# Which engine makes the low parts of the weights in the attention and the mixing of a two-layer hybrid block: one VectorE operation a block in place of two on GpSimd

## The chip, the core and the metric

The kernel runs on one core of a Trainium2 chip. The metric is the device time in microseconds (us) of one execution. Five engines work side by side, each through its own queue in order: TensorE (PE in the profile; its weight loads are PEld), VectorE (DVE), ScalarE (ACT), GpSimd (POOL) and SyncE (SP), which here issues all DMA transfers.

## The reference, cut to what matters

```python
for l in range(2):                                   # x: 512 tokens x 1024
    h = rmsnorm(x, norm_mix[l]);  z = h @ w_in[l]    # 1024 -> 6936 columns, split into 15 parts
    o_nsa  = nsa(...)          # 8 heads of 64; three softmax branches: compressed keys, selected, window
    o_ret  = retention(...)    # 4 heads, chunks of 128
    o_conv = conv_module(...)  # depthwise, 31 taps, 512 channels, layernorm, silu
    merged = sum_n sigmoid(m_g[n]) * (o_n @ w_branch[l, n])
    x = x + merged @ w_out[l]
    h2 = rmsnorm(x, norm_mlp[l])
    x = x + square(relu(h2 @ w_ff1[l])) @ w_ff2[l]   # 1024 -> 4096 -> 1024
return rmsnorm(x, norm_final)
```

All of it is in float32.

## The kernel before

**Products in three passes.** A float32 operand is split into a high part, its copy in the type fp32r, and a low part, the operand minus the high part. A product is then high x high, high x low and low x high. `proj` (L157) does this for one output block of 128 columns: 8 chunks of 128 rows, three matmuls of 128x512 for each, 24 in all; a branch weight has 4 chunks and 12 matmuls.

**Weight blocks.** `wblock` (L153) fetches a block (`raw`, L136, tile `wr`, by a DMA of the SP queue) and splits it (`wsplit`, L142): ScalarE writes the high part `wh` (L145), then another engine writes the low part `wl`. `lo_engine` (L134) says which: GpSimd in two halves (L148), VectorE in one operation (L150). `wr`, `wh` and `wl` have three buffers each, so a block's high part waits until TensorE is done with the block three before.

```python
nc.scalar.activation(h, t, AF.Copy)                              # L145
if lo_engine[0] is nc.gpsimd:
    for k in (slice(0, nk // 2), slice(nk // 2, nk)):
        nc.gpsimd.tensor_sub(l[:, k], t[:, k], f(h[:, k]))       # L148
else:
    nc.vector.tensor_sub(l, t, f(h))                             # L150
```

GpSimd is set at the start, VectorE for one block of the first convolution input (L310), and VectorE for the feed-forward part (L799), with GpSimd again behind it (L819).

**A layer, in order.** Norm and split of x (`norm_split`, L209); convolution inputs and retention (L304 to L438); compressed keys, keys and values (`compress`, L485; L550 to L577); attention (L620 to L760), eight rounds of a head pair's half, each with two branches of scores, softmax and weighted values; mixing of the three branches and the output projection (L762 to L793); feed-forward (L796 to L818).

**What lies inside the attention.** For each branch of a head: scores on TensorE (`sc`), bias and row minimum on VectorE (L712), exponent on ScalarE (L714), the normaliser on VectorE (`gate_over`, L624: L627 to L629, 128x4 elements), scaling on ScalarE (L719), transposes on TensorE (`tp`, L722), the transposed block split by ScalarE (L727) and VectorE (L728, `pt`), then the weighted values on TensorE (`av`). Between them stand independent projections (`fill`, L474, called by `more`, L745): gates (`gate`, L444: projection, L448 on VectorE, tanh on ScalarE) and the retention's branch (`mix`, L456). VectorE also does the convolution there, one tap an operation (`conv_taps`, L329, L338), spread behind other work, and the split queries (L657).

**What sets the order.** The program is recorded through a framework whose scheduler orders the instructions of every engine; `tc.issue_after` binds some of them to others. A change of engine for one operation therefore moves others too. TensorE's work does not change in amount.

Of the kernel before, what the change touches and what calls it, by code (L numbers as in the profile page):

```python
# [66 lines left out]
def block_kernel(ctx: ExitStack, tc: tile.TileContext, a, out):  # L67
    nc = tc.nc
# [18 lines left out]
    def new_pool(name, side="left"):  # L87
        return tc.tile_pool(name=name, bufs=1, side=side, reuse_waits="tile")
# [45 lines left out]
    lo_engine = [nc.gpsimd]  # L134
# [74 lines left out]
    def norm_split(x, gain, first_time=False):  # L209

        pairs, acc = [], None
        for c in range(KC):
            h, l = tl(base, "X", 16, dtype=FR), tl(base, "X", 16, dtype=FR)
            at = nc.scalar.activation(h, x[c], AF.Copy, scale=gain[:, c:c + 1])  # L214
            nc.vector.scalar_tensor_tensor(l, x[c], gain[:, c:c + 1], f(h), op0=OP.mult, op1=OP.subtract)
            pairs.append((h, l))
            if c == (KC - 1 if first_time else 0):
                last = at
        with tc.issue_after(last.ins):
            for c in range(KC):  # L220
                s = tmp()
                if first_time and c < 3:
                    nc.gpsimd.tensor_mul(s, x[c], x[c])
                else:
                    nc.scalar.activation(s, x[c], AF.Square)
                if acc is not None:
                    (nc.vector if c == KC - 1 or first_time else nc.gpsimd).tensor_add(s, s, acc)  # L227
                acc = s
        rs4 = rsqrt_rows(column_sums(acc), 1.0 / D)
        rs = tl(base, "rs", 1)  # L230
        nc.scalar.activation(rs, rows_to_bcast(rs4), AF.Copy)
        return pairs, rs4, rs
# [37 lines left out]
    for l in range(DEPTH):  # L270
# [346 lines left out]
        normed = conv_norm()  # L617


        a2 = open_pools.enter_context(new_pool(f"late{l}"))  # L620
        phase = ExitStack()
        ap = phase.enter_context(new_pool(f"att{l}"))
# [173 lines left out]
        phase = ExitStack()  # L796
        fp = phase.enter_context(new_pool(f"ff{l}"))
        X, rs4, rs = norm_split(xT, par(8, 8))
        lo_engine[0] = nc.vector  # L799
        for q in range(4):  # L800
            A = []
            for m in range(KC):
# [86 lines left out]
```

## Time and profile before

| | us |
|---|---|
| median of 3 runs | 1793.1 |
| lowest and highest run | 1789.49 and 1793.3 |
| the profiled execution's own time | 1793.25 |
| its span, first to last instruction | 1791.5 |

Busy time says how long an engine had an instruction under way; the granted clock (PEclk, or `clock`) is the share of full speed that TensorE was given, 1.00 for 2.4 GHz and 0.50 for 1.2 GHz, averaged over a stretch. Over the whole span it is 0.989. Times of rows are counted from the start of the span. In layer 0 the stretch from 196 to 222 us is the passage from the keys and values into the attention, 222 to 380 us the body of the attention, 380 to 455 us its tail, where the projections between run out, and 455 to 545 us the mixing; in layer 1 the same stretches are 1075 to 1102, 1102 to 1260, 1260 to 1337 and 1337 to 1425 us.

### The profile page before, as it was taken

The numbers are of one execution on the slowest core, as the hardware profiler recorded it, in microseconds if no ns is written. First come the engines' busy times: TensorE is split into PE (matmuls) and PEld (weight loads), VectorE is DVE, ScalarE is ACT, GpSimd is POOL, SyncE is SP. The second block draws the span as 40 slices with busy tenths as digits, with TensorE's granted clock in tenths as the row PEclk, the third lists the DMA queues.
The fourth block names the chain that finished last, engine by engine and source line by source line (L and its number), as shares of the span: only waits on it lengthen the run. The fifth ranks groups of instructions, "written<-read, shape, count | busy, mean of one in ns | idle before, by whom it ended". The sixth has DMA issues, their size and how long they took to land.

```text
span 1791.5 us, 23230 instructions
## 1 busy us (share of the span) xinstructions
PE 1750.2 (98%) x8592; PEld 1469.7 (82%) x8592; DVE 1101.9 (62%) x1979; ACT 775.0 (43%) x1421; POOL 504.8 (28%) x420
## 2 busy tenths in 40 slices
PE   8899899999999999999999999999999999999997
PEld 7788788887888888888898888888778888888886
DVE  6976978776764344434459768878768443434344
ACT  4433466675443232323434344667644442323241
POOL 4454444322581000000255544343327500000000
PEclk9999999999999999999999999999999999999999
DMA  4222623321553232333322232232236332332321
GB/s 166 89 86 64 198 95 107 112 95 65 205 184 105 94 94 94 96 95 101 133 101 89 89 119 92 95 126 98 83 122 227 122 94 95 94 96 93 106 85 69
DMA packets 70801, 195.82 MB, mean 109 GB/s; under 512 B 8944, under 2 KB 9328, under 8 KB 70688
## 3 DMA queue, kind: packets, MB, share of 16 engines
q1 hardware_dynamic: 70688, 194.34, 33.5%
q8 instruction: 68, 1.11, 0.3%
q14 instruction: 45, 0.37, 0.1%
HBM read 177.51 MB, written 19.42 MB: 110 GB/s over the span
## 4 chain that ended last, share of the span: by engine, by line
PE 68%; issue 20%; DVE 10%; ACT 1%; DMA 1%; SPq 0%; POOL 0%; POOLq 0%; DVEq 0%; ACTq 0%
PE mm L109 59%; PE sc L109 3%; PE av L109 3%; DVE yc L338 3%; PE tp L722 2%; PE tp L109 1%; DVE qk L386 1%; DVE XP L500 0%; DVE pc L684 0%; DVE rr L364 0%; DVE QS L657 0%; DVE s L712 0%; DVE pt L728 0%; DVE g L448 0%; DVE kv L563 0%
## 5 line engine op out<-in xcount | busy, mean ns | idle before, releaser
L109 PE MATMUL mm<-X,wh 128*128 128x512 f32 x2432 | 779.5, 396 | 12.5 <-ACT X L214 6.0
L148 POOL TENSOR_TENSOR wl<-wr,wh 128x512 fp32r<-128x512 f32 (+2 forms) x344 | 440.1, 1302 | 542.8 <-ACT wh L145 526.8
L145 ACT ACTIVATE wh<-wr 128x1024 fp32r<-128x1024 f32 (+2 forms) x301 | 296.0, 986 | 650.9 <-PE mm L109 522.1
L109 PEld LDWEIGHTS mm<-X,wh 128*128 128x128 f32 x2432 | 456.0, 190 | 102.2 <-ACT X L214 6.0
L109 PE MATMUL mm<-X,wl 128*128 128x512 f32 x1216 | 480.7, 395 | 0.0
L109 PEld LDWEIGHTS mm<-X,wl 128*128 128x128 f32 x1216 | 230.5, 190 | 45.3
L338 DVE SCALAR_TENSOR_TENSOR yc<-u,ccol,yc 128x512 f32<-128x512 f32 x240 | 213.0, 889 | 1.5
L150 DVE TENSOR_TENSOR wl<-wr,wh 128x1024 fp32r<-128x1024 f32 x129 | 158.1, 1226 | 38.2 <-ACT wh L145 38.2
L109 PE MATMUL mm<-bo,wh 128*128 128x512 f32 x512 | 160.6, 392 | 0.0
L109 PE MATMUL mm<-fa,wh 128*128 128x512 f32 x512 | 160.2, 395 | 0.0
L806 DVE SCALAR_TENSOR_TENSOR t<-mm,rs 128x512 f32<-128x512 f32 x64 | 43.9, 691 | 161.6 <-PE mm L109 156.1
L206 POOL TENSOR_TENSOR n<-n,mhalf 128x4 f32<-128x4 f32 x15 | 17.4, 1159 | 371.9 <-DVE n L204 371.9
L227 POOL TENSOR_TENSOR t<-t,t 128x512 f32<-128x512 f32 x18 | 27.4, 1523 | 333.7 <-DVE wl L150 314.4
L109 PE MATMUL mm<-kv,wh 128*128 128x512 f32 x384 | 119.7, 390 | 0.0
L109 PEld LDWEIGHTS mm<-fa,wh 128*128 128x128 f32 x512 | 96.1, 188 | 23.2
L109 PEld LDWEIGHTS mm<-bo,wh 128*128 128x128 f32 x512 | 96.1, 188 | 19.5
L728 DVE TENSOR_TENSOR pt<-tp,pt 128x256 fp32r<-128x256 f32 (+1 forms) x192 | 71.2, 375 | 65.0 <-ACT pt L727 64.3
L109 PE MATMUL mm<-fa,wl 128*128 128x512 f32 x256 | 100.6, 395 | 0.0
L109 PE MATMUL mm<-bo,wl 128*128 128x512 f32 x256 | 100.0, 391 | 0.0
L714 ACT ACTIVATE s<-s,n 128x128 f32<-128x128 f32 (+3 forms) x128 | 71.3, 558 | 43.9 <-DVE n L712 43.4
L109 PE MATMUL mm<-wh,X 128*128 128x256 f32 (+1 forms) x480 | 90.2, 287 | 0.0
L727 ACT ACTIVATE pt<-tp 128x256 fp32r<-128x256 f32 (+1 forms) x192 | 63.7, 340 | 58.6 <-PE tp L722 42.6
(219 smaller groups left out, 2417.9 us busy)
## 6 DMA issues: line engine op xcount, KB each, us to landing
wr<-in_w_dram SPq DMA_DIRECT2D x128, 512.0 KB, 3.6
wr<-in_w_f_dram SPq DMA_DIRECT2D x87, 512.0 KB, 3.3
wr<-in_w_b_dram SPq DMA_DIRECT2D x48, 256.0 KB, 2.7
wr<-in_w_t_dram SPq DMA_DIRECT2D x16, 512.0 KB, 3.4
gd<-g SPq DMA_DIRECT2D x32, 256.0 KB, 2.0
g<-gd SPq DMA_DIRECT2D x32, 256.0 KB, 4.1
wr<-in_w_o_dram SPq DMA_DIRECT2D x16, 512.0 KB, 3.6
md<-g SPq DMA_DIRECT2D x16, 256.0 KB, 2.9
```

What stands on the lines that cost most here:

```text
L109: return nc.tensor.matmul(o, l, r, start=start, stop=stop)
L145: nc.scalar.activation(h, t, AF.Copy)
L148: nc.gpsimd.tensor_sub(l[:, k], t[:, k], f(h[:, k]))
L150: nc.vector.tensor_sub(l, t, f(h))
L227: (nc.vector if c == KC - 1 or first_time else nc.gpsimd).tensor_add(s, s, acc)
L338: nc.vector.scalar_tensor_tensor(yc[c], x, w, yc[c], op0=OP.mult, op1=OP.add)
L386: nc.vector.tensor_sub(QLr[h][half], pt[nat], f(QHr[h][nat]))
L714: nc.scalar.activation(s, s, AF.Exp, scale=-1.0, bias=mx[:, i:i + 1], accum_out=den[:, i:i + 1])
L722: nc.tensor.transpose(pt[:, k * P:(k + 1) * P], cols[i][:, k * P:(k + 1) * P], ident)
L727: nc.scalar.activation(vh, src, AF.Copy)
L728: low = nc.vector.tensor_sub(vl, src, f(vh))
L806: nc.vector.scalar_tensor_tensor(t, pf, 0.0, rs, op0=OP.max, op1=OP.mult)
```

## The change

`lo_engine` is set to VectorE ahead of the attention instead of ahead of the feed-forward part. Lines 620 to 799 of the kernel before have numbers that are one higher behind the change.

```diff
         normed = conv_norm()
 
 
+        lo_engine[0] = nc.vector
         a2 = open_pools.enter_context(new_pool(f"late{l}"))
         phase = ExitStack()
         ap = phase.enter_context(new_pool(f"att{l}"))
...
         X, rs4, rs = norm_split(xT, par(8, 8))
-        lo_engine[0] = nc.vector
         for q in range(4):
```

On GpSimd 344 instructions of L148 become 112; on VectorE 129 of L150 become 245. The 116 blocks that move, 58 a layer, are 70 of 128x1024 and 46 of 128x512: the queries, all but the first block pair of the retention's mixing, the gates that are computed ahead, the branch weights and the output projection. Instructions of TensorE, ScalarE and SP are the same in number.

On VectorE, layer 0, at the passage into the attention, before (`yc` is a convolution tap, `XP`, `m` belong to the compressed keys, `kv` are keys and values):

```order
L338 SCALAR_TENSOR_TENSOR yc_261<-u_952,ccol,yc_261 128x512 x3
L500 TENSOR_TENSOR XP_1742<-E_1735,pcol 128x16x31
L338 SCALAR_TENSOR_TENSOR yc_261<-u_952,ccol,yc_261 128x512
...
L513 TENSOR_TENSOR m_1687<-m_1687,tp_1670 128x62
L573 SCALAR_TENSOR_TENSOR kv_2068<-mm_1947,n_177,kv_2068 128x4x64
```

and with the change:

```order
L150 TENSOR_TENSOR wl_2100<-wr_2097,wh_2099 128x1024
L338 SCALAR_TENSOR_TENSOR yc_261<-u_952,ccol,yc_261 128x512 x2
L500 TENSOR_TENSOR XP_1742<-E_1735,pcol 128x16x31
L338 SCALAR_TENSOR_TENSOR yc_261<-u_952,ccol,yc_261 128x512
...
L513 TENSOR_TENSOR m_1687<-m_1687,tp_1670 128x62
L150 TENSOR_TENSOR wl_2260<-wr_2257,wh_2259 128x1024
L573 SCALAR_TENSOR_TENSOR kv_2068<-mm_1947,n_177,kv_2068 128x4x64
```

The low parts of the first two queries now stand ahead of the operations on the values (L573); the rest of the order there is as it was.

On VectorE, layer 0, in the tail of the attention, before (`g` is a gate, `pt` a transposed block, `on` the end of a round):

```order
L728 TENSOR_TENSOR pt_4122<-tp_4147,pt_4121 128x2x128
L448 TENSOR_TENSOR g_4525<-mm_4493,rs_179 128x512
L728 TENSOR_TENSOR pt_4122<-tp_4147,pt_4121 128x256
L338 SCALAR_TENSOR_TENSOR yc_263<-u_1476,ccol,yc_263 128x512
L728 TENSOR_TENSOR pt_4235<-tp_4237,pt_4234 128x128
L338 SCALAR_TENSOR_TENSOR yc_263<-u_1476,ccol,yc_263 128x512
L739 TENSOR_TENSOR on_3984<-t_4202,av_3985 64x512
```

and with the change:

```order
L729 TENSOR_TENSOR pt_4096<-tp_4121,pt_4095 128x2x128
L448 TENSOR_TENSOR g_4493<-mm_4462,rs_179 128x512
L150 TENSOR_TENSOR wl_4631<-wr_4628,wh_4630 128x512
L729 TENSOR_TENSOR pt_4096<-tp_4121,pt_4095 128x256
L338 SCALAR_TENSOR_TENSOR yc_263<-u_1476,ccol,yc_263 128x512
L729 TENSOR_TENSOR pt_4208<-tp_4210,pt_4207 128x128
L338 SCALAR_TENSOR_TENSOR yc_263<-u_1476,ccol,yc_263 128x512
L740 TENSOR_TENSOR on_3959<-t_4175,av_3960 64x512
```

A low part has come in right behind the operation that empties a gate's projection (L448), ahead of the next transposed block; the rest is as it was.

## Rows read from the trace of the kernel before

**Rows 1.** The page's first part: busy time, share of the span and number of instructions of each engine.

```profile
PE 1750.2 (98%) x8592; PEld 1469.7 (82%) x8592; DVE 1101.9 (62%) x1979; ACT 775.0 (43%) x1421; POOL 504.8 (28%) x420
```

**Rows 2.** The busy time of each engine in the stretches around the change. Columns: the stretch, its length, then for each engine its busy time with the number of instructions, the granted clock, the share of the DMA engines and GB/s.

```profile
196.00:222.00 26.00, 21.31 (x124) 18.87 (x124) 25.47 (x35) 5.70 (x14) 10.29 (x8) 0.93 0.55 168
222.00:380.00 158.00, 156.48 (x808) 132.19 (x807) 125.28 (x353) 109.20 (x267) 59.02 (x51) 1.00 0.32 104
380.00:455.00 75.00, 71.00 (x351) 58.31 (x350) 51.51 (x134) 44.50 (x109) 20.30 (x16) 0.95 0.22 72
455.00:545.00 90.00, 90.00 (x401) 73.62 (x400) 61.23 (x78) 39.93 (x60) 63.12 (x50) 1.00 0.60 203
...
1075.00:1102.00 27.00, 24.98 (x138) 22.61 (x136) 26.59 (x39) 7.11 (x17) 11.20 (x9) 0.87 0.32 102
1102.00:1260.00 158.00, 157.10 (x807) 132.79 (x807) 125.48 (x356) 107.94 (x265) 58.71 (x51) 1.00 0.32 103
1260.00:1337.00 77.00, 73.00 (x365) 60.19 (x364) 51.38 (x128) 46.98 (x115) 20.65 (x17) 0.96 0.24 81
1337.00:1425.00 88.00, 88.00 (x384) 71.37 (x383) 59.31 (x76) 36.90 (x56) 62.78 (x51) 1.00 0.60 195
```

**Rows 3.** TensorE's waits between 196 and 222 us: who waited for whom, us in total, times, the longest.

```profile
PE mm L109 <- ACT G L575: 4.7, 1, 4.7
```

**Rows 4.** Who waited for GpSimd's low parts (L148) in the whole span: us, times.

```profile
  ACT wh L145: 27.0, 14
  PEld mm L109: 0.6, 3
```

**Rows 5.** GpSimd's low parts by form, in the body (first two rows) and in the tail (last two) of layer 0's attention. Columns: line, engine, operation, tiles, shapes, number | busy us, mean ns of one | idle time before them and its releaser.

```profile
L148 POOL TENSOR_TENSOR wl<-wr,wh 128x512 fp32r<-128x512 f32 x36 | 49.0, 1384 | 74.4 <-ACT wh L145 74.4
L148 POOL TENSOR_TENSOR wl<-wr,wh 128x256 fp32r<-128x256 f32 x12 | 9.1, 777 | 21.9 <-ACT wh L145 21.9
...
L148 POOL TENSOR_TENSOR wl<-wr,wh 128x512 fp32r<-128x512 f32 x12 | 17.0, 1438 | 38.0 <-ACT wh L145 33.2 <-PE tp L722 4.7
L148 POOL TENSOR_TENSOR wl<-wr,wh 128x256 fp32r<-128x256 f32 x4 | 3.3, 846 | 16.9 <-ACT wh L145 16.9
```

**Rows 6.** VectorE's low parts of 128x1024 and, as the nearest operation of 128x512, the low part of an activation in the feed-forward part; whole span, columns as above.

```profile
L150 DVE TENSOR_TENSOR wl<-wr,wh 128x1024 fp32r<-128x1024 f32 x129 | 158.1, 1226 | 38.2 <-ACT wh L145 38.2
...
L113 DVE TENSOR_TENSOR fa<-t,fa 128x512 fp32r<-128x512 f32 x32 | 21.8, 692 | 1.7 <-ACT fa L112 1.7
```

**Rows 7.** Four kinds of VectorE operation in the body of layer 0's attention, columns as above.

```profile
L338 DVE SCALAR_TENSOR_TENSOR yc<-u,ccol,yc 128x512 f32<-128x512 f32 x40 | 34.0, 849 | 0.0
L657 DVE TENSOR_TENSOR QS<-tq,QS 64x512 fp32r<-64x512 f32 x8 | 8.5, 1063 | 0.7 <-ACT QS L656 0.4
...
L627 DVE TENSOR_SCALAR n<-n 128x4 f32<-128x4 f32 x18 | 7.6, 440 | 4.3 <-ACT s L714 4.1
...
L629 DVE SCALAR_TENSOR_TENSOR n<-G,n 128x4 f32<-128x4 f32 x18 | 5.9, 335 | 0.2
```

**Rows 8.** The same four over the whole span: shortest, median and longest in ns, then first and last start in us.

```profile
L338 DVE SCALAR_TENSOR_TENSOR yc<-u,ccol,yc x240: 729/745/1866, 35.3 to 1313.8; 128x512 f32<-128x512 f32 x120
...
L657 DVE TENSOR_TENSOR QS<-tq,QS x16: 684/963/1810, 223.1 to 1231.4; 64x512 fp32r<-64x512 f32 x16
...
L627 DVE TENSOR_SCALAR n<-n x48: 152/170/1254, 230.0 to 1304.5; 128x4 f32<-128x4 f32 x48
...
L629 DVE SCALAR_TENSOR_TENSOR n<-G,n x48: 147/161/1254, 230.6 to 1304.9; 128x4 f32<-128x4 f32 x48
```

**Rows 9.** VectorE's instructions in order of time at the passage into layer 0's attention: start and length in us, engine, line, operation.

```profile
194.41 1.65 DVE L338 SCALAR_TENSOR_TENSOR yc<-u,ccol,yc 128x512 f32<-128x512 f32 x1
196.09 1.64 DVE L563 TENSOR_TENSOR kv<-t,kv 64x512 fp32r<-64x512 f32 x1
...
200.01 2.03 DVE L500 TENSOR_TENSOR XP<-E,pcol 128x496 f32<-128x496 f32 x1
201.96 1.71 DVE L338 SCALAR_TENSOR_TENSOR yc<-u,ccol,yc 128x512 f32<-128x512 f32 x1
203.59 0.97 DVE L500 TENSOR_TENSOR XP<-E,pcol 128x496 f32<-128x496 f32 x1
```

**Rows 10.** VectorE's longest waits in the body of layer 0's attention: who for whom, us in total, times, the longest.

```profile
DVE pt L728 <- ACT pt L727: 15.7, 18, 2.0
DVE s L712 <- PE sc L109: 6.5, 7, 2.9
DVE n L627 <- ACT s L714: 4.1, 5, 1.0
```

**Rows 11.** Stretches of 20 us outside the attention in which VectorE was busy for 17.9 to 18.9 us; columns as in rows 2.

```profile
60.00:80.00 20.00, 18.25 (x93) 14.76 (x91) 18.37 (x29) 11.08 (x20) 11.16 (x10) 1.00 0.25 80
120.00:140.00 20.00, 20.00 (x104) 17.17 (x103) 17.97 (x28) 9.28 (x17) 12.91 (x11) 1.00 0.27 87
940.00:960.00 20.00, 19.46 (x124) 17.55 (x123) 18.12 (x38) 10.89 (x20) 10.13 (x11) 1.00 0.24 79
960.00:980.00 20.00, 19.78 (x97) 16.32 (x96) 17.96 (x23) 6.32 (x10) 11.31 (x8) 1.00 0.28 93
...
1060.00:1080.00 20.00, 20.00 (x144) 19.05 (x142) 18.80 (x20) 12.37 (x20) 10.18 (x8) 1.00 0.49 166
```

## The prediction

> **What bounds the kernel now.** I began with the busy times of the page: TensorE is under way for 98% of the span and VectorE for 62% [rows 1]. That is an average over stages, so the stretches around the change come next [rows 2]. The reader should see three different things there. In the mixing TensorE is busy for all of 90 and all of 88 us: nothing on another engine costs time. In the body of the attention it is busy for 156.5 and 157.1 of 158 us, and VectorE for 125.3 and 125.5 of them, which is 79%: TensorE is the bound, with VectorE not far behind. In the passage into the attention and in its tail TensorE loses time: 26 - 21.3 = 4.7 us and 27 - 25.0 = 2.0 us at the passages, 75 - 71 = 4.0 us and 77 - 73 = 4.0 us in the tails, and the granted clock is 0.93, 0.87, 0.95 and 0.96 there instead of 1.00.
>
> Then I looked at who waits for the low parts that are to move. TensorE's weight loads waited for GpSimd three times, 0.6 us in all; ScalarE waited 27 us in 14 cases for a buffer [rows 4], and it is not the bound. So a faster low part buys nothing by itself. What the change can buy or cost lies on VectorE: what it takes on, what it is freed of, and whether TensorE then waits for it.
>
> **What is moved, and its price.** Each layer moves 35 blocks of 128x1024 and 23 of 128x512. VectorE makes a 128x1024 low part in 1.226 us; for 128x512 I take 0.692 us, the nearest operation of that shape [rows 6]. That is 35 x 1.226 + 23 x 0.692 = 58.8 us a layer on VectorE, 117.6 us in all, in place of two GpSimd operations a block. Where it falls decides.
>
> **What VectorE is freed of.** Some VectorE operations take much longer in some places than in others. In the body a convolution tap takes 849 ns on average [rows 7] against a median of 745; the 128x4 steps L627 and L629 take 440 and 335 ns [rows 7] against medians of 170 and 161, with single cases of 1254 ns; a split query takes 1063 ns against a shortest of 684 [rows 8]. A step on four columns that lasts 1.25 us is not at work; it is as long as GpSimd's halves of 1.38 us on average [rows 5], and I read it as held up by them. With no low parts on GpSimd in the body this goes: 40 x 0.104 + 18 x 0.270 + 18 x 0.174 + 8 x 0.379 = 15.2 us of VectorE time a layer. The bounds are 0 (they are held by something else) and 15.2; I take it whole, since both the short and the long values of the same shape are there.
>
> **Body of the attention.** Per layer 36 / 2 = 18 large and 12 / 2 = 6 small blocks lie there [rows 5]: 18 x 1.226 + 6 x 0.692 = 26.2 us. Net of the 15.2 us VectorE goes from 125.3 to 136.3 of 158 us, 86%. What does TensorE lose at such a load? The nearest rows are the stretches with VectorE at 90%: 17.97 of 20 us with no loss of TensorE and 17.96 with 0.22 us; over all five stretches of 90 to 94% the loss is 1.75 + 0 + 0.54 + 0.22 + 0 = 2.51 us, 0.50 each [rows 11]. For 158 us that is 7.9 x 0.50 = 4.0 us against the 1.5 us lost now, so +2.5 us a layer at the high end; the two nearest rows give 7.9 x 0.11 = 0.9 us, no more than now. The low end is -1.5 us, all of today's loss gone. I take 0. If this cover is gone, each us that VectorE is late is a us of TensorE's.
>
> **Passage into the attention.** TensorE stands still for 4.7 us in layer 0, waiting for the gates' tanh on ScalarE (L575), which frees the accumulators [rows 3]; that stands behind VectorE's operations on the values (L573), and VectorE is busy for 25.5 of 26 us [rows 2]. The order of the change puts two large low parts ahead of the first L573: + 2 x 1.226 = 2.5 us. Four operations ahead of it are slow now: two taps of 1.65 and 1.71 us, an L563 of 1.64 us and an L500 of 2.03 us whose twin takes 0.97 [rows 9]. Beside 0.745 us for a tap [rows 8], 0.69 us for the L563 (from the split query of the same shape, shortest 684 ns [rows 8]) and 0.97 us, the excess is 0.90 + 0.96 + 0.95 + 1.06 = 3.9 us. So 3.9 - 2.5 = 1.4 us off the wait. Bounds: -4.7 us (the wait goes) and +2.5 us (the excess stays). For layer 1, where the loss is 2.0 us, I take 0.
>
> **Tail.** 6 large and 2 small blocks a layer [rows 5] are 8.7 us more on VectorE, which has 51.5 of 75 us [rows 2]. There is room, but here the chain transposes, L727, L728, weighted values is bare, and the order puts the low parts between its links, each behind an L448. Bounds: 0 (each lies under a gate's 24 matmuls) and 8.7 us a layer (all on the chain). As most stand behind a gate's projection while another runs, I take one of the eight on the chain: 8.7 / 8 = 1.1 us a layer, 2.2 us in all.
>
> **Mixing.** 16 small and 8 large are at most 16 x 0.692 + 8 x 1.226 = 20.9 us on top of 61.2 of 90 us. TensorE is full there; I cost it at nothing, and 4.5 x 0.50 = 2.3 us a layer [rows 11] if the cover fails.
>
> On the splitting of the work: the Trainium skill (Perfetto Trace Analysis, Optimizing Scalar/DVE Operations) says that where such an engine is not saturated but makes others wait, breaking an operation up can let work finish sooner; the change does the opposite, one operation a block for two. By that rule TensorE could begin a block half an operation earlier before, and the sum would be that of the third rival; by the row of three waits in all it is nothing, and the sum goes by the row.
>
> **The sum.** Against the profiled execution, 1793.25 us, which is 0.15 us above the median: - 1.4 + 0 + 2.2 + 0 gives **1794.0 us**, no change. About 0.2%, 3.6 us, is what a measurement of this kernel can tell from none.
>
> **The rivals.** First, faster: the relief reaches TensorE where it stands still. The passages lose 4.7 + 2.0 us, and the clock there costs 26 x 0.07 + 27 x 0.13 = 5.3 us more [rows 2]; all of it gone is -12 us, 1781, and half, **1787 us**. For it: the slow VectorE operations stand directly ahead of the L573 for which TensorE waits [rows 3, 9]. Against it: the two new low parts stand there too.
>
> Second, slower: VectorE becomes the bound in the body. Its idle time there is 158 - 125.3 = 32.7 us, 26.3 of them waits for ScalarE and TensorE [rows 10]; its low parts wait for ScalarE as well, 38.2 us for 129, 0.30 us each [rows 6], 7.1 us for 24. If none of these 39.8 us is filled by the new work, VectorE needs 136.3 + 39.8 = 176 us, 18 us a layer more than TensorE, 1830. It decides where less than 18 / 39.8 = 45% is filled; at a third filled it is 136.3 + 26.5 = 162.8 us, 4.8 us a layer, and with it **1804 us**. For it: the queue is in order, and a low part that waits for its high part holds every score and transposed block behind it. Against it: the longest group is 18 waits of 0.9 us on average, so one low part of 1.2 us fills one whole, and the rows at 90% lose little [rows 11].
>
> Third, each of the 116 blocks makes TensorE wait for the half that it once had early, 1.226 / 2 = 0.61 us: at most +71 us, **1864 us**. Rows 4 speak against it. That the change doesn't do what it says is excluded by the order: 232 instructions have left GpSimd and 116 have come to VectorE.
>
> **How the numbers follow.** No change 0.39, the first rival 0.30, the second 0.29, the third 0.02. Faster by over 0.2% is the first, 0.30; slower the second and third, 0.31. The forecast's own range is 1790 to 1797 us; the range for 8 in 10 takes in most of the first two rivals and leaves out their ends, some 0.1 each way: 1784 to 1807 us.
>
> **What would show it.** Right: VectorE busy for about 136 us of a body that is still 158 us, L627 and L629 near 0.17 us and taps near 0.75 us there; TensorE's wait for L575 near 3.3 us; two tails together longer by some 2 us. Wrong: a body of over 161 us with TensorE waiting for L713 (the row minimum, L712 before) or L729; a passage without a wait and a clock of 1.00 there; taps as slow as before.

## The result, and the profile after

The median after is **1804.7 us** (5 runs, 1803.95 to 1809.72) against 1793.1 us before: ratio **1.0071**, 95% interval 1.0059 to 1.0083. That is slower. The forecast's time, 1794.0 us, did not come; the time of its second rival, 1804 us, did, and lies in the range. The profiled execution took 1803.95 us with a span of 1802.2 us, 10.7 us over that of before.

Three marks on TensorE's queue say where: the first scores with compressed keys (`sc<-kc`), the first product of the mixing (`mm<-os`), the first product that reads activations of the feed-forward part (`mm<-fa`). "Mixing" between the last two marks is longer than the 90 us of [rows 2]: it takes in the norm and the first quarter of the feed-forward's first products. All times in this table are from TensorE's rows of the two timelines, in us.

| | before | after | difference |
|---|---|---|---|
| start to first scores, layer 0 | 222.8 | 220.5 | -2.3 |
| attention, layer 0 and 1 | 236.5, 236.1 | 239.7, 241.3 | +3.2, +5.2 |
| mixing, layer 0 and 1 | 134.0, 134.3 | 135.9, 135.9 | +1.9, +1.6 |
| last `mm<-fa` of layer 0 to first scores of layer 1 | 287.4 | 288.0 | +0.6 |

This adds up to 10.2 of the 10.7 us. The attention carries 8.4, the mixing 3.5, and the passages give 1.7 back.

Not all of that is the change, for each length carries TensorE's clock as well. In before, the granted clock is 0.50 for 6.8 us of each attention; in after it is so for 6.8 us of layer 1's and not in layer 0's. The stretch in layer 0 of before:

```profile
438.60:445.40 6.80, 6.33 (x28) 5.64 (x26) 2.85 (x9) 1.60 (x5) 0.00 (x0) 0.50 0.07 28
```

At half speed 6.8 us cost some 3.4 (an estimate). With such stretches taken out the attentions are 6.6 and 5.2 us longer than before. The 2.3 us at the start are not the change alone either: the wait in the passage is 1.5 us shorter, but TensorE also comes to it 0.9 us earlier, and at 80 us, far ahead of the change, it had the lower clock for 6.8 us before and for 3.4 us after.

The page's first part of after [rows 1 of before]: GpSimd loses 285 us of busy time, VectorE gains only 30, though its low parts (L150) take 116.8 us more. Its other operations are shorter by 72 us in sum; the rest is overlap of neighbouring operations, which busy time counts once.

```profile
PE 1750.1 (97%) x8592; PEld 1466.2 (81%) x8592; DVE 1131.9 (63%) x2095; ACT 776.6 (43%) x1421; POOL 220.0 (12%) x188
```

The stretches of after, as [rows 2] (the last two shifted to where the tail and the mixing of layer 1 now lie):

```profile
196.00:222.00 26.00, 22.78 (x132) 20.15 (x131) 24.09 (x43) 8.49 (x18) 0.31 (x1) 0.93 0.66 197
222.00:380.00 158.00, 154.66 (x795) 130.12 (x795) 127.64 (x366) 106.02 (x258) 0.94 (x3) 1.00 0.32 104
380.00:455.00 75.00, 67.48 (x345) 54.78 (x344) 56.56 (x145) 46.74 (x115) 0.00 (x0) 1.00 0.18 60
455.00:545.00 90.00, 88.27 (x393) 71.80 (x392) 66.48 (x98) 37.41 (x57) 9.75 (x6) 1.00 0.62 202
...
1102.00:1260.00 158.00, 156.48 (x800) 131.56 (x799) 129.71 (x366) 103.65 (x255) 0.94 (x3) 1.00 0.33 107
1260.00:1346.00 86.00, 79.20 (x394) 64.92 (x393) 61.62 (x153) 51.91 (x126) 0.00 (x0) 0.96 0.22 69
1346.00:1436.00 90.00, 88.27 (x387) 71.52 (x386) 66.56 (x98) 36.43 (x55) 11.54 (x7) 1.00 0.60 194
```

In the body VectorE has hardly more to do than before, 127.6 against 125.3 us, while TensorE has lost 1.8 us; in the tail TensorE is idle 7.5 of 75 us (4.0 before), and the mixing has a gap of 1.7 us where it had none. TensorE's waits of after in layer 0 from 222 to 460 us:

```profile
PE sc L109 <- DVE n L713: 5.6, 6, 1.6
PE av L109 <- DVE pt L729: 2.5, 4, 0.7
PE av L109 <- ACT pt L728: 1.2, 2, 0.7
PE mm L109 <- DVE u L590: 0.9, 1, 0.9
PE av L109 <- DVE on L740: 0.7, 1, 0.7
```

and of before in the same stretch:

```profile
PE sc L109 <- DVE n L712: 3.1, 5, 1.0
PE av L109 <- DVE on L739: 1.0, 1, 1.0
PE av L109 <- DVE pt L728: 0.5, 1, 0.5
PE av L109 <- ACT pt L727: 0.5, 1, 0.5
```

10.9 us against 5.1 (and 0.2 in a row left out): the waits for the row minimum and for transposed blocks have grown. One of them in the timeline of after, VectorE first (start, length, engine, line):

```profile
338.79 1.22 DVE L150 TENSOR_TENSOR wl<-wr,wh 128x1024 fp32r<-128x1024 f32 x1
339.92 0.55 DVE L713 CUSTOM_DVE_ANT_0 s<-sc,bias 128x384 f32<-128x384 f32 x1
340.39 0.08 DVE L713 DVE_READ_ACCUMULATOR2_ANT n<- 128x1 f32 x1
...
338.55 0.47 PE L109 MATMUL av<-pt,kv 128*128 128x512 f32 x1
340.53 0.44 PE L109 MATMUL sc<-kv,QS 128*128 128x128 f32 x2 [1.51 <-DVE n L713]
```

The low part stands ahead of the row minimum that empties a score accumulator; TensorE stands still until the minimum is done. The low part did not wait for its high part first: all of VectorE's waits for `wh` in the body are 2.1 us. In the whole attention of layer 0 TensorE waits 12 times for VectorE, 9.6 us; in 6 of them, 5.6 us, a low part stands directly ahead of the operation that it waits for. In layer 1 it is 5 of 10 waits and 4.6 of 6.7 us. The low part itself is under way for 3.0 and 2.1 us of this time. Before, no low part stands there.

### The profile page after: what moved, and what is told of

Same layout as the page of the kernel before. It is cut to its first block, busy times and chain, and to the rows that moved or that the text cites. A ratio compares the mean times of both kernels' runs of the same rounds, so it can differ in the third digit from the quotient of the medians.

```text
span 1802.2 us, 23028 instructions
## 1 busy us (share of the span) xinstructions
PE 1750.1 (97%) x8592; PEld 1466.2 (81%) x8592; DVE 1131.9 (63%) x2095; ACT 776.6 (43%) x1421; POOL 220.0 (12%) x188
## 4 chain that ended last, share of the span: by engine, by line
PE 67%; issue 20%; DVE 11%; ACT 2%; DMA 0%; SPq 0%; POOLq 0%; POOL 0%; DVEq 0%; ACTq 0%
PE mm L109 58%; PE sc L109 3%; PE av L109 3%; DVE yc L338 2%; PE tp L723 1%; PE tp L109 1%; DVE wl L150 1%; DVE pt L729 1%; DVE kv L563 1%; DVE qk L386 1%; DVE s L713 1%; ACT s L720 1%; DVE XP L500 0%; ACT wh L145 0%; DVE rr L364 0%
## 5 line engine op out<-in xcount | busy, mean ns | idle before, releaser
L150 DVE TENSOR_TENSOR wl<-wr,wh 128x1024 fp32r<-128x1024 f32 (+1 forms) x245 | 274.7, 1122 | 43.7 <-ACT wh L145 43.6
L338 DVE SCALAR_TENSOR_TENSOR yc<-u,ccol,yc 128x512 f32<-128x512 f32 x240 | 193.4, 807 | 1.3
L148 POOL TENSOR_TENSOR wl<-wr,wh 128x512 fp32r<-128x512 f32 (+2 forms) x112 | 151.8, 1378 | 171.1 <-ACT wh L145 171.1
L729 DVE TENSOR_TENSOR pt<-tp,pt 128x256 fp32r<-128x256 f32 (+1 forms) x192 | 70.4, 374 | 39.3 <-ACT pt L728 38.7
L817 DVE TENSOR_TENSOR yc<-yc,mm 128x512 f32<-128x512 f32 x32 | 22.1, 689 | 105.7 <-PE mm L109 105.7
```

What stands on the lines that cost most here:

```text
L338: nc.vector.scalar_tensor_tensor(yc[c], x, w, yc[c], op0=OP.mult, op1=OP.add)
L729: low = nc.vector.tensor_sub(vl, src, f(vh))
L817: nc.vector.tensor_add(xT[m], xT[m], pf)
```

## The experiments

An accumulator is a buffer that TensorE writes its products into; the scores have two, the transposes two, the projections three. Theory 1: a low part that stands in VectorE's queue ahead of an operation that frees an accumulator makes TensorE wait. Theory 2: VectorE has too much work in all. Theory 3: the order drawn up anew costs by itself. Lengths are measured between the marks above, in the profiled execution; "at 0.50" is how many us of each attention had the lower clock, of which about half is lost. The last column says whether TensorE waits 1.7 us for L608 (the convolution norm's multiplications) in the mixing of layer 0 and of layer 1. Ratios are to before as it ran beside each kernel, with 95% intervals; V is VectorE, G GpSimd.

| kernel | low parts in attention, mixing | us | ratio | attention 0, 1 | at 0.50 | mixing 0, 1 | wait for L608 |
|---|---|---|---|---|---|---|---|
| before | G, G | 1793.1 | 1 | 236.5, 236.1 | 6.8, 6.8 | 134.0, 134.3 | no, no |
| after | V, V | 1804.7 | 1.0071 | 239.7, 241.3 | 0, 6.8 | 135.9, 135.9 | yes, yes |
| mixing only | G, V | 1796.9 | 1.0029 [1.0018, 1.0040] | 236.3, 236.0 | 6.8, 6.8 | 135.9, 136.0 | yes, yes |
| attention only | V, G | 1807.0 | 1.0082 [1.0068, 1.0096] | 242.4, 240.1 | 6.8, 3.4 | 136.9, 136.7 | yes, yes |
| none | none | 1776.6 | 0.9915 [0.9900, 0.9929] | 230.7, 231.0 | 0, 0 | 135.2, 135.2 | 0.3 us, 0.3 us |
| halves | V | 1802.2 | 1.0053 [1.0036, 1.0069] | 242.4, 244.9 | 6.8, 10.2 | 135.8, 134.9 | yes, no |
| unread, VectorE | V | 1800.3 | 1.0049 [1.0034, 1.0064] | 242.9, 237.1 | 10.2, 3.4 | 134.4, 135.9 | no, yes |
| unread, GpSimd | G | 1798.6 | 1.0042 [1.0029, 1.0054] | 236.1, 236.6 | 0, 0 | 137.1, 134.4 | yes, no |
| norm later | V | 1812.5 | 1.0123 [1.0103, 1.0142] | 239.7, 240.9 | 0, 6.8 | 137.7, 138.7 | yes, yes |
| after, no taps | V | 1788.8 | 0.9983 [0.9973, 0.9994] | 236.0, 232.7 | 0, 0 | 133.7, 135.2 | no, no |
| before, no taps | G | 1779.4 | 0.9930 [0.9911, 0.9948] | 228.3, 228.2 | 0, 0 | 134.1, 133.6 | no, no |
| two queries | G but four blocks | 1796.7 | 1.0030 [1.0020, 1.0041] | 236.6, 233.6 | 3.4, 3.4 | 136.7, 136.9 | yes, yes |
| mean copied | V | 1823.7 | 1.0180 [1.0162, 1.0197] | 248.4, 249.6 | 5.5, 11.8 | 136.2, 136.3 | no, no |
| bound behind scores | V | 1834.0 | 1.0237 [1.0222, 1.0253] | 260.6, 257.8 | 18.6, 6.9 | 136.6, 136.6 | no, no |

**Which stage: mixing only, attention only.** VectorE is set ahead of the mixing, or for the attention alone:

```diff
-        lo_engine[0] = nc.vector        # mixing only: not ahead of the attention
...
+        lo_engine[0] = nc.vector        # attention only: nc.gpsimd
         phase = ExitStack()
         pp = phase.enter_context(new_pool(f"post{l}"))
```

> VectorE makes the low parts from the mixing on; the attention keeps GpSimd. In the changed kernel TensorE waits 1.7 us a layer in the mixing for the convolution's norm (L608 on VectorE), and the stretch from the first product of the mixing to the first of the feed-forward's second half is 1.9 and 1.6 us longer. Theory 1 (a low part that stands in VectorE's queue ahead of an operation that frees an accumulator makes TensorE wait): this stays, about +3.5 us, 1795 to 1797, with the wait for L608 in the trace. Theory 2 (VectorE has too much work): VectorE is at 74% in the mixing, so nothing, 1791 to 1794. Theory 3 (the order of the instructions, drawn up anew, costs it by itself): no number, but the wait need not be that for L608.

> VectorE makes the low parts in the attention; the mixing has GpSimd again. Between the first compressed score and the first product of the mixing the changed kernel is 3.2 and 5.2 us longer, its passage of layer 0 about 2 us shorter. Theory 1: these stay, +6 to +9 us, 1798 to 1801, and the mixing's +3.5 us go. Theory 2 gives the same sign here, with VectorE busy for 128 to 130 of 158 us of the body. If the time is that of the changed kernel, 1804, the mixing costs nothing and the split by stretches is wrong.

The attention is as long as before with GpSimd there, and 4 to 6 us longer with VectorE: its loss comes with its own low parts. The mixing is longer in both, with either engine: my split was wrong there, and its loss is not VectorE's load. Attention only, at 1807.0 us, lies above every time expected of it.

**What the low parts cost on each engine: none, unread on VectorE, unread on GpSimd.**

```diff
+        if lo_engine[0] is None:                  # none
+            nc.scalar.activation(h, t, AF.Copy)
+            return h, h
...
-        return h, l
+        return (h, h) if unused[0] else (h, l)    # unread, on either engine
```

> Leaves out the low parts of the weights in the attention and the mixing: the high part is used in their place, so TensorE does the same number of products, and neither GpSimd nor VectorE makes a low part there. Against the kernel before this takes away GpSimd's hold on VectorE (15 us of VectorE's time a body) and nothing else; against the changed kernel it takes away 58.8 us of VectorE a layer. Theories 1 and 2: the attention is no longer than before, the passage shorter: 1783 to 1791, that is 14 to 21 us under the changed kernel. Theory 3: with the order drawn up anew here too, it stays above before, 1796 or more.

> As the kernel without low parts of weights in the attention and the mixing (1776.6 us), but VectorE makes every one of the 116 all the same and nothing reads it: the products take the high part in its place. If TensorE loses time because VectorE's queue is longer and what stands behind a low part comes late (theories 1 and 2): back up by 24 to 28 us, 1800 to 1805. If it loses time because it has to wait for the low part itself: it stays at 1776 to 1780.

> The kernel before, in which GpSimd still makes the 116 low parts of the attention and the mixing, but the products take the high part in their place, so that nobody reads them. Without the low parts the time was 1776.6 us, before 1793.2. If the 16.6 us that the kernel before pays for its low parts are GpSimd's hold on VectorE: 1789 to 1794, with the 128x4 steps of the normaliser still up to 1.25 us long. If they are the waits of a product for its own low part, or a block's start put off by them: 1775 to 1781.

None leaves out the low parts, the unread pair makes them and leaves out their use. Low parts that nobody reads cost 1800.3 - 1776.6 = 23.7 us on VectorE and 1798.6 - 1776.6 = 22.0 us on GpSimd. So a product's wait for its own part is not what costs, and in this pair GpSimd costs nearly what VectorE costs. A good part of none's gain is the clock: over the span 0.995 was granted instead of 0.989, some 11 of the 18 us between the profiled spans (1791.5 x 0.011 - 1773.3 x 0.005 = 10.8, an estimate).

Where the products read them the two kernels stand 11.6 us apart, the unread pair 1.7. How much of the 11.6 us is the engine and how much the order is not shown: unread on GpSimd makes the same operations as before on every engine, in another order, and takes 6.4 us more than before beside it (1792.2 us), and 4.6 us more than the most expected of it. The body of layer 0 without low parts; columns as in [rows 2]:

```profile
222.00:380.00 158.00, 157.71 (x813) 133.11 (x812) 109.88 (x359) 109.54 (x274) 0.94 (x3) 1.00 0.33 105
```

the same with unread ones on VectorE:

```profile
222.00:380.00 158.00, 156.17 (x799) 130.75 (x798) 127.94 (x371) 104.89 (x259) 0.94 (x3) 1.00 0.32 104
```

and with unread ones on GpSimd:

```profile
222.00:380.00 158.00, 155.49 (x803) 131.30 (x802) 122.90 (x344) 106.10 (x262) 59.53 (x51) 1.00 0.32 105
```

GpSimd's low parts add 13.0 us to VectorE's busy time though VectorE makes none; its own add 18.1. Where they add, in the kernel with unread parts on GpSimd (taps and the first step of the normaliser):

```profile
L339 DVE SCALAR_TENSOR_TENSOR yc<-u,ccol,yc 128x512 f32<-128x512 f32 x39 | 34.3, 879 | 0.0
...
L629 DVE TENSOR_SCALAR n<-n 128x4 f32<-128x4 f32 x18 | 7.4, 424 | 4.9 <-ACT s L716 4.7
```

and that step without low parts:

```profile
L631 DVE TENSOR_SCALAR n<-n 128x4 f32<-128x4 f32 x20 | 3.0, 168 | 6.2 <-ACT s L718 6.1
```

The hold is GpSimd's, as predicted, and it is shown by taking the low parts away. It reaches TensorE too. In unread on GpSimd, two operations on the compressed keys' probabilities (L686) last 2.52 us together, 0.29 us each where GpSimd makes no low parts, while two of its halves run; the row minimum stands behind them:

```profile
341.98 2.55 POOL L149 TENSOR_TENSOR wl<-wr,wh 128x512 fp32r<-128x512 f32 x2 [3.72 <-ACT wh L146]
342.15 2.52 DVE L686 TENSOR_TENSOR pc<-pc,n 128x128 f32<-128x128 f32 x2
345.20 0.44 PE L109 MATMUL sc<-kv,QS 128*128 128x128 f32 x2 [2.09 <-DVE n L714]
```

A low part can thus delay what frees an accumulator from either engine: on VectorE by standing ahead of it, on GpSimd by holding what stands ahead of it.

**Load or place: halves, no taps, bound behind the scores.** Halves makes VectorE's low part in two operations. The pair without taps leaves out the taps of the convolution's attention share (all but the first of a channel), in after and in before. The last one keeps VectorE's work and moves it: a low part of the attention goes behind the last row minimum recorded.

```diff
-        if lo_engine[0] is nc.gpsimd:
+        if lo_engine[0] is nc.gpsimd or halved[0]:         # halves
...
+        todo[:] = [x for x in todo if x[1] == 0]           # no taps
         late_taps = len(todo)
...
+            if last_min:                                   # bound behind scores
+                behind.enter_context(tc.issue_after(last_min[-1].ins))
             nc.vector.tensor_sub(l, t, f(h))
```

> As the changed kernel, but each low part on VectorE in the attention and the mixing in two halves, 0.69 us for a half of 128x1024 instead of 1.22 us for the whole, so some 7 us more of VectorE a layer. Theory 1: what stands ahead of a score or a transposed block is shorter, and others can come between: 1797 to 1802. Theory 2: more work on the loaded engine: 1806 to 1812.

> As the changed kernel, but leaves out the convolution taps that lie in the attention (all but the first tap of a channel), about 60 a layer, 45 us of VectorE a layer. Theory 2 (VectorE's total): with VectorE at some 100 of 158 us in the body the difference to the kernel before without the same taps shrinks to the mixing's 3.5 us. Theory 1 (what stands directly behind a low part comes late by up to 1.2 us, full queue or not): a difference of 8 us or more remains.

> As the kernel before, without the same taps: the base for the run above. TensorE is the bound, so a few us under the kernel before, 1783 to 1792, since fewer operations stand between the scores and the transposed blocks.

> The changed kernel, but a low part that is made inside the attention is bound behind the last row minimum (L713) of the branch recorded before it: VectorE's work is the same, its place is not. The low parts now stand two and three together ahead of the transposed blocks (L729) and seldom ahead of a row minimum. Theory 1 (what stands in VectorE's queue ahead of an operation that frees an accumulator makes TensorE wait): the waits for L713 of 2.9 and 2.7 us in layer 0 go under 1, the waits for L729 rise above 2, and the time moves by over 2 us one way or the other; which way depends on whether two low parts in a row are covered at the transposed blocks (1798 to 1801) or not (1807 to 1815). Theory 2 (too much work in all on VectorE): no change, 1803 to 1806, with waits where they were.

Without taps VectorE is busy 107.4 us of after's body and 93.8 of before's, and the two still stand 9.3 us apart: a VectorE with 50 us to spare does not save the change, which speaks against theory 2. The attention carries it, 7.7 and 4.5 us, at full clock in both kernels. It is not theory 1 in its plain form alone: of TensorE's waits in layer 0's attention, 6.9 us against 0.9, 2.8 are for ScalarE's high part of a transposed block. With the same load in another place the time rises by 29 us, which theory 2 excludes. But theory 1 was wrong in what it expected of that run; its waits from 215 to 475 us:

```profile
PE mm L109 <- DVE wl L154: 5.2, 7, 1.9
PE sc L109 <- DVE n L717: 5.0, 7, 2.8
...
PE av L109 <- ACT pt L733: 1.4, 3, 0.5
```

The waits for the minimum did not go (L717 is the minimum, L154 the low part): three low parts in a row, 2.95 us, can now stand ahead of the next round's first minimum, and blocks now come too late for their own products. The granted clock falls too, to 0.96 in 215 to 380 us, and layer 0's attention holds 22 more matmuls, for the first scores come at 214.1 us. Halves, at the edge of what theory 1 expected, cannot be told from after (their intervals overlap), and its attention is no shorter, with the clock's share out 239.0 and 239.8 us against 239.7 and 237.9; what it gains lies ahead of layer 1's attention, 4.2 us (283.8 against 288.0 us). At three waits in its attentions both halves of a block stand one behind the other, the longest of 2.25 us. So the place counts more than the load, and neither shorter pieces nor this binding finds a good one.

**The mixing: norm later, two queries, mean copied.**

```diff
-            if m == 1:
+            if m == 2:                                     # norm later
                 next(normed, None)
...
+        tqs.append(query(1)); lo_engine[0] = nc.gpsimd     # two queries, VectorE until here
...
-            pm = rows_to_bcast(mean, "mm")                 # mean copied
+            pm = tmp()
+            nc.scalar.activation(pm, rows_to_bcast(mean, "mm"), AF.Copy)
```

> As the changed kernel, but the last step of the convolution's norm is recorded behind the third product of the mixing instead of the second. By the order this puts L464 of two products ahead of the four L608 on VectorE, as in the kernel before. If the wait of 1.7 us a layer for L608 is one of order alone: 3 to 4 us under the changed kernel, 1800 to 1802. If it comes from the low parts on VectorE: no gain, 1803 to 1806.

> The kernel before, but VectorE makes the low parts of the first two queries of a layer alone, at the passage into the attention (four blocks in all); GpSimd makes the others as before. If the passage gains what it gained with the change (the first scores of the compressed keys began at 220.5 us in place of 222.8), and the loss in the attention comes from the low parts within it: 1789 to 1792 us, attention and mixing as long as before (236 and 134 us a layer). If an order drawn up anew costs by itself: 1794 or more, with a longer mixing.

> The changed kernel, but ScalarE copies the mean of the convolution's layernorm out of its accumulator, and the four subtractions (L608) read the copy. If the mixing is 1.6 to 1.9 us a layer longer because the four subtractions hold that accumulator while the products' accumulators wait behind them: TensorE's wait of 1.7 us for L608 goes, the mixing is 134 to 134.5 us, 1800 to 1802 us in all. If the low parts on VectorE make the mixing longer in another way: no change, 1803 to 1806.

Two queries is the telling one. Its wait for L575 is as short as with the change (3.2 us); its first scores come at 220.3 us, but those of mixing only, where the wait is 4.7 us as before, come at 220.9, so this mark does not show the gain. The attention is no longer than before, and the mixing, all on GpSimd, is 2.7 and 2.6 us longer. The edit does one thing more than it was meant to: it records the second query ahead of the attention instead of inside the first round, so the four blocks' change of engine is not shown to suffice by itself. Its waits from 455 to 620 us:

```profile
PE mm L109 <- DVE yc L608: 1.7, 1, 1.7
PE mm L109 <- DVE os L113: 0.6, 1, 0.6
```

Unread on GpSimd has both cases in one kernel: layer 0 waits for its L608 and takes 137.1 us, layer 1 does not and takes 134.4. Before, VectorE did two L464 (which empty the products' accumulators) ahead of the four L608, 2.48 us long; after, L608 comes first. This is theory 3, and in the mixing it is what costs. In the attention it is not excluded: with the clock's share out, that of unread on GpSimd is 3.0 and 3.9 us longer than before's, with the same operations on the same engines. Norm later put the L464 ahead again, but then low parts ahead of L608, and TensorE waited as long; at 1812.5 us it is slower than either case expected.

Mean copied was meant to show the mechanism and took the wrong operand: L608 multiplies by the broadcast of the deviation, and the subtractions that read the mean are L597. ScalarE made the copy late, behind the end of a round, so the subtractions began at 458.49 us instead of 446.78. The norm's sums, which stand ahead of the first product of the mixing in after as well, came late by it, and TensorE waited 7.7 us a layer. First after, then mean copied:

```profile
446.78 2.47 DVE L597 TENSOR_TENSOR yc<-yc,mm 128x512 f32<-128x512 f32 x4
...
457.75 0.60 ACT L595 ACTIVATE t<-mm 128x512 f32<-128x512 f32 x1
458.49 2.50 DVE L598 TENSOR_TENSOR yc<-yc,t 128x512 f32<-128x512 f32 x4
466.69 1.87 PE L109 MATMUL mm<-ones,u 128*128 128x1 f32 x8 [7.70 <-DVE u L602]
```

Even so it bears on the mixing, which has no wait for L608 there. Of its 136.2 and 136.3 us, 4.8 and 5.2 us had the lower clock; with half of them out it is 133.8 and 133.7 us, as long as before, though VectorE makes the low parts. Bound behind scores, also without that wait, is 134.9 us twice in the same way. So low parts on VectorE cost the mixing next to nothing beside that wait. What norm later has beyond its waits (2.5 and 2.8 of 3.7 and 4.4 us) stays open.

Beyond every time expected of them lie also none (1776.6 us against 1783 at least), before without taps (1779.4 against 1783), mean copied and bound behind scores. No version that does the whole work beats before.

## Why the prediction was wrong in its forecast and right in its range

**Passage: right.** The sum had 1.4 us off the wait for L575 in layer 0, to 3.3 us, from four slow operations that get fast. From 196 to 222 us of after:

```profile
PE mm L109 <- ACT G L575: 3.2, 1, 3.2
```

That is 1.5 us. The first scores begin 2.3 us earlier, of which 0.9 lie ahead of the wait; layer 1 has 0.6 us more where I took 0.

**What VectorE is freed of: right, and a little short.** After, body of layer 0 [rows 7 for before]:

```profile
L338 DVE SCALAR_TENSOR_TENSOR yc<-u,ccol,yc 128x512 f32<-128x512 f32 x40 | 29.7, 743 | 0.0
L150 DVE TENSOR_TENSOR wl<-wr,wh 128x1024 fp32r<-128x1024 f32 x18 | 21.9, 1217 | 1.6 <-ACT wh L145 1.6
...
L658 DVE TENSOR_TENSOR QS<-tq,QS 64x512 fp32r<-64x512 f32 x6 | 4.1, 687 | 0.2
L150 DVE TENSOR_TENSOR wl<-wr,wh 128x512 fp32r<-128x512 f32 x6 | 4.1, 687 | 0.5 <-ACT wh L145 0.5
...
L628 DVE TENSOR_SCALAR n<-n 128x4 f32<-128x4 f32 x18 | 2.7, 162 | 0.6 <-ACT s L715 0.5
...
L630 DVE SCALAR_TENSOR_TENSOR n<-G,n 128x4 f32<-128x4 f32 x18 | 2.6, 158 | 0.2
```

40 x 0.106 + 18 x 0.278 + 18 x 0.177 + 8 x 0.376 = 15.4 us, priced at 15.2; the low parts 26.0, priced at 26.2. Yet VectorE's busy time is 127.6 us, not 136.3. Two more lines were held before that I had not listed (L677 and L684, 596 and 537 ns before, 422 and 285 after, 2.2 us); the stretch now holds fewer queries and transposed blocks; and neighbouring operations overlap by some 0.08 us, which busy time counts once.

**Body of the attention: wrong. This is the failing step.** I put VectorE's busy share against TensorE's loss in stretches outside the attention [rows 11] and read 0. Those stretches have no scores with two accumulators behind a row minimum. The load I feared did not come (81% instead of 86%), and TensorE lost time all the same: a low part that stands ahead of L713 or L729 is what it waits for in half of its waits for VectorE. The attention with its tail was costed at 1.1 us a layer and measured +3.2 and +5.2. In the tail of layer 0 alone TensorE's idle time rose by 3.5 us. Over the attention of layer 0 its waits grew by 5.6 us, the clock gave some 3.4 back, and 1.0 us has no row. In layer 1 the waits grew from 4.8 to 8.0 us (1102 to 1345 us), the clock had the same share, and 2.0 have no row. How much of this is the place of the low parts and how much a worse order stays open: waits with a low part directly ahead are 5.6 and 4.6 us.

**Mixing: mis-sized.** Costed at 0 with 2.3 us a layer as the bound, it measured +1.9 and +1.6, of which 1.7 us is the wait for L608. It comes not from VectorE's load but from the order of L608 and L464, which no term of the sum had.

**The second rival** had the time, 1804, and the sentence that describes the wait (a low part holds every score and transposed block behind it). Its arithmetic was another: VectorE never became the bound (30.4 us idle in the body), and the low parts did not wait for their high parts. It was right about the place and wrong about the reason, and part of the 11.6 us is the mixing's, which it did not have. That its 1804 us was measured is a coincidence, and that the range held is luck: it reaches that far up only because of this rival. The third, halves, fell: after's list of waits above has none of TensorE's products for a low part of its own, its weight loads waited 0.5 us for them in the whole span, and low parts that nobody reads cost nearly as much.

## What to carry to other kernels

Before moving work onto an engine with idle time, look at what stands behind it in that engine's queue: if that frees one of two accumulators, the price can be the length of the operation, also where the queue has room. A change of engine draws up a new order, and here another order of the same operations on the same engines cost 6.4 us; measure such a move alone before blaming the engine. Look at the granted clock of each stage before comparing its lengths. Work on GpSimd is not free for VectorE: take it away once to see what it costs there.

## What the runs showed of the hardware

GpSimd's operations hold some VectorE operations and not others. In the body of before:

```profile
L728 DVE TENSOR_TENSOR pt<-tp,pt 128x256 fp32r<-128x256 f32 x39 | 16.3, 418 | 13.9 <-ACT pt L727 13.8
L448 DVE TENSOR_TENSOR g<-mm,rs 128x512 f32<-128x512 f32 x14 | 9.6, 686 | 0.7 <-PE mm L109 0.5
...
L684 DVE TENSOR_TENSOR pc<-pc,n 128x128 f32<-128x128 f32 x6 | 3.0, 537 | 0.0
L628 DVE RECIPROCAL n<-n 128x4 f32<-128x4 f32 x18 | 2.9, 170 | 0.2
...
L677 DVE TENSOR_TENSOR pc<-pc,n 128x256 f32<-128x256 f32 x4 | 2.4, 596 | 0.1
```

and of after (the two lines that got faster):

```profile
L678 DVE TENSOR_TENSOR pc<-pc,n 128x256 f32<-128x256 f32 x4 | 1.7, 422 | 0.1
...
L685 DVE TENSOR_TENSOR pc<-pc,n 128x128 f32<-128x128 f32 x6 | 1.5, 285 | 0.0
```

L728 and L448, one input of which is an accumulator, take 418 and 686 ns there and 418 and 689 after; the reciprocal L628, with one input, takes 170 and 165; L684 and L677, with both inputs in SBUF (the on-chip memory that the tiles lie in), get faster by 252 and 174 ns. But L627, with one input too, was held (440 against 162 ns). The Trainium skill (SBUF — State Buffer, Who interferes with whom) says that a VectorE operation with two SBUF inputs contends with a GpSimd operation that reads SBUF, and one with a single SBUF input only in certain modes. The trace agrees with it in these five lines; which mode L627 ran in no row shows.

After a long stop TensorE ran at the lower clock. In the kernel with the copied mean, three stretches: ahead of the wait of 7.7 us, right behind it, and the next.

```profile
450.00:458.50 8.50, 8.50 (x43) 7.18 (x42) 2.76 (x6) 3.37 (x7) 0.00 (x0) 1.00 0.42 121
466.50:473.00 6.50, 6.31 (x19) 5.34 (x20) 0.30 (x2) 0.00 (x0) 1.01 (x1) 0.50 0.48 163
473.50:480.00 6.50, 6.50 (x32) 5.28 (x31) 5.42 (x9) 1.74 (x3) 0.00 (x0) 1.00 0.24 81
```

The granted clock is 0.50, 1.2 GHz, for the 6.5 us after the wait, and 19 matmuls are done in it where the next 6.5 us have 32: 13 of some 0.23 us. So the wait costs about 3 us more than its own length, an estimate from these rows.
